# Loading the memory into the query projection's sum buffers, and two weighted values in another bank: a decoder block on one core

## The chip, the core and the metric

The kernel runs on one core of a Trainium2 chip. The core has a matrix engine (PE, which loads weights and multiplies), a vector engine (DVE), a scalar engine (ACT), GpSimd (POOL) and a sync engine (SP) that issues transfers. Each engine works its own instructions in order, and they meet at semaphores. Matrix results go to PSUM, eight banks of 128 x 512 float32; everything else lies in SBUF, 128 partitions wide. The metric is the device time of one execution in microseconds, less being better.

## The reference

One decoder block on 512 tokens of width 1024, in float32. A pooling mixer and a differential attention run on the same normed input, are gated and projected back (`w_out`). Then the tokens attend to a memory of 256 rows, and a squared-ReLU MLP follows. The part that the change touches:

```
x = x + mixed @ w_out[l]
hc = rms_norm(x, g_cross[l])
mem_n = rms_norm(mem, g_mem[l])
q = (hc @ w_cq).reshape(B, S, CROSS_HEADS, CROSS_HEAD_DIM)
kv = (mem_n @ w_ckv).reshape(B, M, 2, CROSS_HEADS, CROSS_HEAD_DIM)
k, v = kv[:, :, 0], kv[:, :, 1]
s = jnp.einsum('bshd,bmhd->bhsm', q, k) * CROSS_HEAD_DIM ** -0.5
p = jax.nn.softmax(s, axis=-1)
o = jnp.einsum('bhsm,bmhd->bshd', p, v).reshape(B, S, D_MODEL)
x = x + o @ w_co
```

with 4 heads of width 256.

## The kernel before

Activations lie transposed: 8 blocks of 128 features by 512 tokens. Every product is made from split operands: a value is rounded to a high part (`split`, line 116, a cast on ACT) and the remainder is a low part (line 117, a subtraction on DVE); `mm3` (lines 110 to 112) multiplies high by high, low by high and high by low. Weights pass through a ring: `load` fetches a block of 512 KB into one of three buffers `wraw` (SP's queue, line 154), `prep` splits it into `whi` and `wlo`, three buffers each, and PE multiplies. A block's split starts when PE has left the buffer three blocks earlier.

The order on PE is the order of the code. Work that belongs to a later moment is put off with `after(steps, fn)`: `tick` counts products, and `run_due` issues `fn` when its step has come. The order on ACT, DVE, POOL and SP is set by a scheduler from the code and its own estimates; each of these engines then works strictly in that order. Tags such as `tmp` (10 buffers) or `mraw` (3 in the middle part) are rings of buffers: a new tile waits until the work on the one that it replaces has ended.

The stages around the change:

- The output projection (`projection("out", ...)`): eight blocks of `wm`, m = 0 to 7. The first three sums lie in the banks `sc` and take five of their eight products early; `settle` stands between: it closes the pool of the attention's tiles, opens the pool of the middle part (tags `mraw` and `mfac`) on the same space, loads the residual rows `res` (tag `vr`) and puts off `mem_in` by 16 steps. The blocks 3 to 7 use the two banks `acc` in turn; `done_out` adds a sum to its residual row (`residual`, line 584, the eviction that frees the bank) and squares it (`accumulate`, lines 265 to 269).
- `mem_in`: the memory in four pieces of 2 x 256 columns. Each is scaled by the gain into a high part (line 272, ACT) and a low part (line 273, DVE), in buffers `s`, and its squares are summed (`ssm`, lines 265 to 269). The sum is split, and 20 steps later `stats` sums it over the partitions on PE (`rstd_full`, lines 242 and 243, and `rstd_rows`, lines 257 and 258) and takes the inverse root.
- `mem_k` and `mem_v`: keys and values of the memory, with the blocks of `wckv`.
- `cross_query`: the query projection by a seven-product scheme; some of its weights are sums of blocks, which `load` makes by one load on SP into `mraw` and a second, accumulating one on POOL (line 170).
- `cross_scores`, `cross_transpose`, `cross_out` by head. `cross_out(h)` makes two weighted values (dc = 0, 1), each summed in a bank over the memory's two halves, and splits each into `xg` (the eviction). PE does heads 1, 0, 3 in a row, with head 2's scores and head 3's transposes between 1 and 0; head 2's values follow inside the following projection (`w_co`).

The bank `av` (one) holds sums of the value projection and of the attention; nothing uses it after the attention.

Of the kernel before, what the change touches and what calls it, by code (L numbers as in the profile page):

```python
# [17 lines left out]
P = 128  # L18
T = 512
D = 1024  # L20
# [31 lines left out]
def block_kernel(ctx: ExitStack, tc: tile.TileContext, x0g, xT, memT, wv, wm, wst, wcq, wdn, wckv, wpool, vecs, csts, idn, gfin, out):  # L52
    nc = tc.nc
# [16 lines left out]
    def nm(s):  # L70
        uid[0] += 1
        return f"{s}_{uid[0]}"
# [6 lines left out]
    def sb(tag, shape, bufs, dt=F32):  # L79
        if tag in MID_TAGS and not late:  # L80
            return mid["pool"].tile(shape, dt, tag=tag, name=nm(tag), bufs=bufs)
        p = apool if tag in EARLY_TAGS else late["pool"] if tag in LATE_TAGS else pool
        return p.tile(shape, dt, tag=tag, name=nm(tag), bufs=bufs)

    def tmp(dt=F32):
        return sb("tmp", [P, T], 10, dt)
# [4 lines left out]
    def pair(tag, bufs):  # L91
        return sb(tag, [P, 2, T], bufs, F32R)

    def ps(tag, bufs):
        return psum.tile([P, T], F32, tag=tag, name=nm(tag), bufs=bufs)

    def acc():
        return ps("acc", 2)
# [10 lines left out]
    def mm3(o, lh, ll, rh, rl, start, stop):  # L109
        nc.tensor.matmul(o, lh, rh, start=start, stop=False)  # L110
        nc.tensor.matmul(o, lh, rl, start=False, stop=False)  # L111
        nc.tensor.matmul(o, ll, rh, start=False, stop=stop)  # L112


    def split(hi, lo, src, eng=V):
        S.copy(hi, src)  # L116
        eng.tensor_tensor(lo, src, f(hi), op=ALU.subtract)  # L117
# [117 lines left out]
    def split_sq(sq, w, eng=V):  # L235
        hi = tmp(F32R)[:, :w]
        lo = tmp(F32R)[:, :w]
        split(hi, lo, sq, eng)
        return hi, lo
# [5 lines left out]
    def rstd_full(sp, scratch, w=T):  # L245
        o = ps("tr", 2)[:, :w]
        bcast_sum(o, *sp)
        r = sb("rstd", [P, w], 1) if w == T else sb("mrstd", [P, w + 48], 1)[:, :w]
        rsqrt(r, o, 1.0 / D, scratch, tmp()[:, :w])
        return r  # L250

    def rstd_rows(sp, n):
        hi, lo = sp
        o = ps("tr", 2)
        for i in range(n):
            c = slice(i * P, (i + 1) * P)
            nc.tensor.matmul(o[:, 2 * i:2 * i + 2], hi[:, c], ones[:, :2], start=True, stop=False)
            nc.tensor.matmul(o[:, 2 * i:2 * i + 2], lo[:, c], ones[:, :2], start=False, stop=True)
        r = sb("rrow", [P, 16], 2)[:, :2 * n]
        rsqrt(r, o[:, :2 * n], 1.0 / D, sb("rscr", [P, 8], 4)[:, :2 * n], sb("rscr", [P, 8], 4)[:, :2 * n])  # L260
        return r

    def accumulate(ss, k, src, w=T):
        if k == 0:
            S.activation(ss, src, AF.Square)
        else:
            sq = tmp()[:, :w]
            S.activation(sq, src, AF.Square)
            V.tensor_tensor(ss, ss, sq, op=ALU.add)

    def scaled(hi, lo, src, g):
        S.activation(hi, src, AF.Copy, scale=g)
        V.scalar_tensor_tensor(lo, src, g, f(hi), op0=ALU.mult, op1=ALU.subtract)
# [5 lines left out]
    def after(steps, fn, *args):  # L279
        heapq.heappush(due, (clock[0] + steps, uid[0], fn, args))  # L280
        uid[0] += 1
# [11 lines left out]
    def flush():  # L293
        while due:
            clock[0] = max(clock[0], due[0][0])
            run_due()
# [48 lines left out]
    st = {}  # L345
# [258 lines left out]
    def mem_in():  # L604
        mg = {}
        sm = sb("ssm", [P, M], 1)
        for k2 in range(KC // 2):
            t = tmp()
            nc.gpsimd.dma_start(t, memT[:, 2 * k2:2 * k2 + 2, :])
            pr = pair("s", 6)  # L610
            for kk in range(2):
                k = 2 * k2 + kk
                c = slice(kk * M, (kk + 1) * M)
                scaled(pr[:, 0, c], pr[:, 1, c], t[:, c], vec[:, G_MEM + k:G_MEM + k + 1])
                accumulate(sm, k, t[:, c], M)
                mg[k] = (pr[:, 0, c], pr[:, 1, c])
        st["mg"] = mg
        sp = split_sq(sm, M)

        def stats():  # L620
            st["mrstd"] = rstd_full(sp, sm, M)
            st["mrow"] = rstd_rows(sp, MT)

        after(STATM, stats)
# [97 lines left out]
    def settle():  # L722
        flush()
        early.close()
        mid["pool"] = middle.enter_context(tc.tile_pool(name="mid", bufs=1))
        for m in range(KC):
            res[m] = sb("vr", [P, T], 8)
            nc.sync.dma_start(res[m], xT[:, m, :])
        after(MEMIN, mem_in)

    projection("out", mixed, EARLY, LATE, done_out, settle)
    sp1 = split_sq(ss1, T)

# [46 lines left out]
    def cross_out(h):  # L780
        pt = st["pt", h]
        for dc in range(2):
            o = acc()
            m = 2 * h + dc
            c = slice((m % 4) * P, (m % 4) * P + P)
            for i in range(MT):
                vh, vl = st["mv", m // 4, i]
                mm3(o, vh[:, c], vl[:, c], pt[0][:, i, :], pt[1][:, i, :], i == 0, i == MT - 1)
            pr = pair("xg", 8)
            split(pr[:, 0, :], pr[:, 1, :], o)  # L790
            cross_o[m] = (pr[:, 0, :], pr[:, 1, :])
# [90 lines left out]
    flush()  # L882
    cross_scores(3, "sc", 3)
    cross_out(1)
    cross_scores(2, "sc", 3)
    cross_transpose(3)
    cross_out(0)
    cross_out(3)
    after(2, cross_transpose, 2)
    after(7, cross_out, 2)  # L890
# [206 lines left out]
```

## Time and profile before

| | |
|---|---|
| runs | 720.0, 724.2 and 723.87 us, median 723.87 |
| profiled execution | 721.91 us, its span 720.1 us |
| granted TensorE clock, mean | 0.997 |
| moved by transfers | 94.78 MB, 132 GB/s in the mean |

The profile records one execution. Its times are microseconds from the span's start; a row of the timeline has start, length, engine, line, operation, the tile written and those read, and in brackets how long the engine had been idle and what ended that. A line is often that of a helper, so the tiles tell which step a row belongs to. `SPq` is a transfer's issue; the transfer itself lasts longer, up to its landing.

### The profile page before, as it was taken

To read this page: it belongs to the slowest core of one execution; us is meant where nothing else is said; L and a number is where in the kernel's file an instruction comes from. 1 tells how busy PE (TensorE), PEld (TensorE's weight loads), DVE (VectorE), ACT (ScalarE), POOL (GpSimd) and SP (SyncE) were. 2 spreads that over 40 slices of the span, in tenths; PEclk is the share of its full clock that TensorE was granted. 3 is DMA by queue.
4 is the path that set the end of the run, shared out by engine and by line. 5 is a ranking of instruction groups with operands and counts; after the bars stand their busy time and mean duration, and the time that the engine had idled before them with its cause. 6 is when DMAs were issued, how large, how long until landed. Compare 5 with 4: busy or idle time off the path is not lost.

```text
span 720.1 us, 10711 instructions
## 1 busy us (share of the span) xinstructions
PE 706.0 (98%) x4108; PEld 619.9 (86%) x4108; DVE 506.2 (70%) x818; ACT 425.1 (59%) x719; POOL 72.5 (10%) x67
## 2 busy tenths in 40 slices
PE   8999999999999999999999999999999999999995
PEld 6888788788879889997889988899889998899884
DVE  7597989986397989893786953688337864478633
ACT  7398998677376864572668742377215752257522
POOL 0044111634200000000100000000000000000000
PEclk9999999999999999999999999999999999999998
DMA  8433133134934436222934652168315672043211
GB/s 315 152 118 117 61 102 117 59 103 162 268 115 153 166 129 178 76 88 91 269 108 118 200 152 87 45 191 240 112 59 168 138 250 87 29 119 118 87 59 58
DMA packets 28130, 94.78 MB, mean 132 GB/s; under 512 B 3216, under 2 KB 3344, under 8 KB 28080
## 3 DMA queue, kind: packets, MB, share of 16 engines
q1 hardware_dynamic: 24688, 82.18, 33.1%
q0 software_dynamic: 3248, 11.67, 8.8%
q8 instruction: 32, 0.52, 0.3%
q10 hardware_dynamic: 144, 0.26, 0.1%
q14 instruction: 18, 0.15, 0.1%
HBM read 89.90 MB, written 2.10 MB: 128 GB/s over the span
## 4 chain that ended last, share of the span: by engine, by line
PE 81%; ACT 7%; DVE 6%; DMA 3%; issue 2%; POOL 1%; SPq 0%; DVEq 0%; POOLq 0%; ACTq 0%
PE acc L110 11%; PE acc L112 11%; PE acc L111 11%; PE sc L110 10%; PE sc L112 10%; PE sc L111 10%; PE tr L110 4%; PE tr L112 4%; PE tr L111 4%; DMA tmp<-memT 2%; ACT whi L116 1%; PE sc L397 1%; ACT tmp L459 1%; PE sc L399 1%; DVE wlo L117 1%
## 5 line engine op out<-in xcount | busy, mean ns | idle before, releaser
L116 ACT CAST whi<-wraw 128x1024 fp32r<-128x1024 f32 (+1 forms) x88 | 91.1, 1035 | 98.8 <-PE tr L112 50.8
L117 DVE TENSOR_TENSOR wlo<-wraw,whi 128x1024 fp32r<-128x1024 f32 (+1 forms) x88 | 108.1, 1228 | 39.8 <-ACT whi L116 38.4
L110 PE MATMUL acc<-xg,whi 128*128 128x512 f32 x200 | 80.1, 401 | 0.0
L112 PE MATMUL acc<-xg,wlo 128*128 128x512 f32 x200 | 78.2, 391 | 0.0
L111 PE MATMUL acc<-xg,whi 128*128 128x512 f32 x200 | 77.9, 390 | 0.0
L807 DVE TENSOR_TENSOR tmp<-sc,tmp 128x512 f32<-128x512 f32 x70 | 47.2, 687 | 11.4 <-PE sc L112 11.0
L110 PE MATMUL sc<-mix,whi 128*128 128x256 f32 (+1 forms) x184 | 54.8, 298 | 0.0
L116 ACT CAST whi<-mraw 128x1024 fp32r<-128x1024 f32 x34 | 35.5, 1050 | 32.6 <-PE sc L111 11.0
L112 PE MATMUL sc<-mix,wlo 128*128 128x256 f32 (+1 forms) x184 | 54.1, 294 | 0.0
L111 PE MATMUL sc<-mix,whi 128*128 128x256 f32 (+1 forms) x184 | 54.0, 293 | 0.0
L117 DVE TENSOR_TENSOR wlo<-mraw,whi 128x1024 fp32r<-128x1024 f32 x34 | 41.3, 1222 | 11.2 <-ACT whi L116 10.9
L170 POOL DMA_DIRECT2D mraw<-wst x16 | 13.8, 862 | 332.6 <-DMA mraw<-wst 203.1
L934 DVE SCALAR_TENSOR_TENSOR vr<-acc,sums,vr 128x512 f32<-128x512 f32 x16 | 12.0, 751 | 50.1 <-PE acc L112 50.1
L112 PEld LDWEIGHTS acc<-xg,wlo 128*128 128x128 f32 x200 | 37.5, 188 | 8.3
L110 PEld LDWEIGHTS acc<-xg,whi 128*128 128x128 f32 x200 | 37.6, 188 | 7.1
L111 PEld LDWEIGHTS acc<-xg,whi 128*128 128x128 f32 x200 | 37.7, 188 | 7.0
L116 ACT CAST mhl<-wraw 128x1024 fp32r<-128x1024 f32 x18 | 18.9, 1052 | 38.5 <-PE tr L111 27.4
L112 PEld LDWEIGHTS sc<-mix,wlo 128*128 128x128 f32 x184 | 34.6, 188 | 1.1
L110 PEld LDWEIGHTS sc<-mix,whi 128*128 128x128 f32 x184 | 34.6, 188 | 1.0
L111 PEld LDWEIGHTS sc<-mix,whi 128*128 128x128 f32 x184 | 34.5, 187 | 1.1
L117 DVE TENSOR_TENSOR mhl<-wraw,mhl 128x1024 fp32r<-128x1024 f32 x18 | 22.0, 1224 | 13.8 <-ACT mhl L116 13.8
L110 PE MATMUL sc<-s,whi 128*128 128x256 f32 x112 | 31.4, 281 | 0.0
(321 smaller groups left out, 2163.6 us busy)
## 6 DMA issues: line engine op xcount, KB each, us to landing
wraw<-wm SPq DMA_DIRECT2D x36, 512.0 KB, 3.3
wraw<-wdn SPq DMA_DIRECT2D x32, 512.0 KB, 5.0
mraw<-wst SPq DMA_DIRECT2D x24, 512.0 KB, 4.5
wraw<-wckv SPq DMA_DIRECT2D x16, 512.0 KB, 3.2
mraw<-wst POOLq DMA_DIRECT2D x16, 512.0 KB, 6.9
wraw<-wst SPq DMA_DIRECT2D x16, 512.0 KB, 3.2
mraw<-wcq SPq DMA_DIRECT2D x6, 512.0 KB, 3.9
s<-s SPq DMA_DIRECT2D x8, 256.0 KB, 3.7
```

Of the source, the lines that this page charges most:

```text
L110: nc.tensor.matmul(o, lh, rh, start=start, stop=False)
L111: nc.tensor.matmul(o, lh, rl, start=False, stop=False)
L112: nc.tensor.matmul(o, ll, rh, start=False, stop=stop)
L116: S.copy(hi, src)
L117: eng.tensor_tensor(lo, src, f(hi), op=ALU.subtract)
L170: nc.gpsimd.dma_start(r, part(key, then), accum_op=ALU.add)
L397: nc.tensor.matmul(o[i], xg[k][0][:, tb], wh[:, c], start=k == 0, stop=False)
L399: nc.tensor.matmul(o[i], xg[k][1][:, tb], wh[:, c], start=False, stop=False)
L459: S.activation(e[:, :n], e[:, :n], AF.Exp, bias=mn, scale=-1.0, accum_out=sm[:, c:c + 1])
L807: V.tensor_tensor(u[new], o, u[old], op=ALU.add)
L934: V.scalar_tensor_tensor(y, o, sums[:, 2 * NT + t:2 * NT + t + 1], y, op0=ALU.mult, op1=ALU.add)
```

## The change

The memory's transposed input is loaded in two pieces of 512 KB instead of four of 256 KB. The loads are issued from `settle`, on SP's queue, into two buffers of the tag `mraw`, instead of from `mem_in`, on POOL's queue, into four buffers `tmp`. `mem_in` takes its pieces from those two. And `cross_out` puts the first value of head 0 and the second of head 3 into the bank `av`, the other six into the banks `acc` as before.

```diff
@@ mem_in
         for k2 in range(KC // 2):
-            t = tmp()
-            nc.gpsimd.dma_start(t, memT[:, 2 * k2:2 * k2 + 2, :])
+            t = st["mem"][k2 // 2][:, k2 % 2 * T:(k2 % 2 + 1) * T]
             pr = pair("s", 6)
@@ settle
             nc.sync.dma_start(res[m], xT[:, m, :])
+        st["mem"] = [sb("mraw", [P, D], 3) for _ in range(2)]
+        for j, t in enumerate(st["mem"]):
+            nc.sync.dma_start(t, memT[:, 4 * j:4 * j + 4, :])
         after(MEMIN, mem_in)
@@ cross_out
-            o = acc()
+            o = ps("av", 1) if (h, dc) in ((0, 0), (3, 1)) else acc()
```

What it does to the order of the engines' work, at three places. In the rows, a tile's number tells its buffers apart and has no other meaning; it differs between the two kernels for the same tile, and line numbers of the changed kernel are up to three higher or lower. `x2` stands for two equal instructions in a row.

First, SP's queue in the output projection. Before:

```order
L154 DMA wraw_1845<-wm 128x1024
L154 DMA wraw_1867<-wm 128x1024
L154 DMA mraw_2693<-wcq 128x1024
L154 DMA mraw_2734<-wcq 128x1024
L154 DMA mraw_2795<-wcq 128x1024
L154 DMA wraw_1947<-wm 128x1024
L154 DMA wraw_2037<-wm 128x1024
L154 DMA wraw_2072<-wckv 128x1024
```

Now:

```order
L154 DMA wraw_1845<-wm 128x1024
L154 DMA wraw_1867<-wm 128x1024
L730 DMA mraw_1909<-memT 128x1024
L730 DMA mraw_1910<-memT 128x1024
L154 DMA mraw_2689<-wcq 128x1024
L154 DMA wraw_1951<-wm 128x1024
L154 DMA wraw_2033<-wm 128x1024
L154 DMA mraw_2730<-wcq 128x1024
L154 DMA wraw_2068<-wckv 128x1024
L154 DMA mraw_2791<-wcq 128x1024
```

The memory's loads stand where two of the three query weights stood; those two follow later, each ahead of a block of key weights. In both kernels the first load into `mraw` waits for the last work on the space that the pool takes over, a product of the gates on POOL (line 523). In the kernel now the second and third query weights reuse the memory's buffers, and so wait for ACT's last square of each.

Second, ACT from the last gated value (`mix`) on; `whi_1847`, `whi_1869` are the weights of the output blocks m = 3 and 4, the fourth and fifth. Before:

```order
L116 CAST mix_1819<-s_1679 128x512
L116 CAST whi_1847<-wraw_1823 128x1024
L265 ACTIVATE ss_1822<-vr_1893 128x512
L116 CAST whi_1869<-wraw_1845 128x1024
L268 ACTIVATE tmp_1930<-vr_1895 128x512
L116 CAST whi_1949<-wraw_1867 128x1024
L268 ACTIVATE tmp_1943<-vr_1897 128x512
L272 ACTIVATE s_1977<-tmp_1975,vx_67 128x256
L265 ACTIVATE ssm_1974<-tmp_1975 128x256
```

Now:

```order
L116 CAST mix_1819<-s_1679 128x512
L272 ACTIVATE s_1979<-mraw_1909,vx_67 128x256
L265 ACTIVATE ssm_1978<-mraw_1909 128x256
L272 ACTIVATE s_1979<-mraw_1909,vx_67 128x256
L272 ACTIVATE s_1988<-mraw_1909,vx_67 128x256 x2
L116 CAST whi_1847<-wraw_1823 128x1024
L272 ACTIVATE s_1999<-mraw_1910,vx_67 128x256 x2
L272 ACTIVATE s_2010<-mraw_1910,vx_67 128x256 x2
L265 ACTIVATE ss_1822<-vr_1893 128x512
L116 CAST whi_1869<-wraw_1845 128x1024
```

The memory's scaling has moved from behind three weight casts to ahead of the first of them. Seven of the eight squares of the memory are not in these rows: they come after the third cast, in one piece.

DVE, from the first eviction of the projection (`vr_1893`) on. Before:

```order
L584 TENSOR_TENSOR vr_1893<-sc_1829,vr_1893 128x512
L117 TENSOR_TENSOR wlo_1848<-wraw_1823,whi_1847 128x1024
L584 TENSOR_TENSOR vr_1895<-sc_1851,vr_1895 128x512
L117 TENSOR_TENSOR wlo_1870<-wraw_1845,whi_1869 128x1024
L269 TENSOR_TENSOR ss_1822<-ss_1822,tmp_1930 128x512
L584 TENSOR_TENSOR vr_1897<-sc_1873,vr_1897 128x512
L117 TENSOR_TENSOR wlo_1950<-wraw_1867,whi_1949 128x1024
L269 TENSOR_TENSOR ss_1822<-ss_1822,tmp_1943 128x512
L273 SCALAR_TENSOR_TENSOR s_1977<-tmp_1975,vx_67,s_1977 128x256
```

Now, from the memory's first low part on:

```order
L273 SCALAR_TENSOR_TENSOR s_1979<-mraw_1909,vx_67,s_1979 128x256 x2
L584 TENSOR_TENSOR vr_1893<-sc_1829,vr_1893 128x512
L273 SCALAR_TENSOR_TENSOR s_1988<-mraw_1909,vx_67,s_1988 128x256 x2
L117 TENSOR_TENSOR wlo_1848<-wraw_1823,whi_1847 128x1024
L273 SCALAR_TENSOR_TENSOR s_1999<-mraw_1910,vx_67,s_1999 128x256
L584 TENSOR_TENSOR vr_1895<-sc_1851,vr_1895 128x512
```

Four low parts of the memory and an eviction stand ahead of the low part of the fourth block's weights (`wlo_1848`); before, the memory's first low part came after six rows of weights and evictions and two of squares.

Third, ACT's evictions (`xg`) of the weighted values of heads 0 and 3, in the order of PE's products; ahead of them a high part of head 3's transposed weights (`mfac`) and an exponential of head 2. Before:

```order
L116 CAST mfac_3486<-tr_3495 128x2x256
L760 ACTIVATE tmp_3478,small_3476<-sc_3462,small_3475,rrow_2287 128x256 x2
L116 CAST xg_3509<-acc_3502 128x512
L116 CAST xg_3519<-acc_3512 128x512
L116 CAST xg_3529<-acc_3522 128x512
L116 CAST xg_3539<-acc_3532 128x512
```

Now:

```order
L116 CAST mfac_3482<-tr_3491 128x2x256
L762 ACTIVATE tmp_3474,small_3472<-sc_3458,small_3471,rrow_2283 128x256 x2
L116 CAST xg_3505<-av_3498 128x512
L116 CAST xg_3515<-acc_3508 128x512
L116 CAST xg_3525<-acc_3518 128x512
L116 CAST xg_3535<-av_3528 128x512
```

Nothing moves in the order here; two sums change their bank. With two banks `acc` in turn, head 3's first value stood in the bank of head 0's first; now it stands in that of head 1's second.

## The prediction

> **What bounds the kernel now.** I read the page first, then the list of PE's waits, then PE's timeline around each of them that the change can touch, then ACT, DVE, POOL and SP at those places. The first rows are of the page: span, busy time by engine, the chain by engine.
>
> ```profile
> span 720.1 us, 10711 instructions
> ...
> PE 706.0 (98%) x4108; PEld 619.9 (86%) x4108; DVE 506.2 (70%) x818; ACT 425.1 (59%) x719; POOL 72.5 (10%) x67
> ...
> PE 81%; ACT 7%; DVE 6%; DMA 3%; issue 2%; POOL 1%; SPq 0%; DVEq 0%; POOLq 0%; ACTq 0%
> ```
>
> PE is the bound: all that the other engines do can cost at most 720.1 - 706.0 = 14.1 us, start and end included. The chain gives 3% to DMA, and the one transfer of this change is 10.9 us of it; but a chain follows what was late, not what PE lost. What PE lost stands in its timeline (start, length, and in brackets the idle time with its releaser):
>
> ```profile
> 187.23 0.39 PE L110 MATMUL acc<-mix,whi 128*128 128x512 f32 x1
> ...
> 187.69 0.39 PE L112 MATMUL acc<-mix,wlo 128*128 128x512 f32 x1
> ...
> 197.99 0.40 PE L112 MATMUL acc<-mix,wlo 128*128 128x512 f32 x1
> 198.90 0.47 PE L110 MATMUL acc<-mix,whi 128*128 128x512 f32 x1 [0.52 <-DVE vr L584]
> 199.21 0.40 PE L111 MATMUL acc<-mix,whi 128*128 128x512 f32 x1
> ...
> 206.44 0.39 PE L112 MATMUL acc<-mix,wlo 128*128 128x512 f32 x1
> 207.46 0.38 PE L242 MATMUL tr<-tmp,ones 128*128 128x256 f32 x1 [0.63 <-ACT tmp L116]
> 207.96 0.38 PE L243 MATMUL tr<-tmp,ones 128*128 128x256 f32 x1
> ...
> 323.61 0.40 PE L112 MATMUL acc<-mfac,mix 128*128 128x512 f32 x1
> 324.88 0.50 PE L110 MATMUL acc<-mfac,mix 128*128 128x512 f32 x1 [0.87 <-DVE xg L117]
> 325.22 0.40 PE L111 MATMUL acc<-mfac,mix 128*128 128x512 f32 x1
> ```
>
> From 187.23 to 187.69 are two steps, so a 512-column matmul starts every 0.23 us (a 256-column one takes half, 0.12). Starts further apart than that are lost time: at 198.90, 0.91 - 0.23 and 0.31 - 0.23, together 0.76 us; at 207.46, 1.02 - 0.23 and 0.50 - 0.12, together 1.17 us; at 324.88, 1.27 - 0.23 and 0.34 - 0.23, together 1.15 us. These 3.08 us are all that the two edits can reach.
>
> Behind the first two stands one transfer. ACT and DVE, with POOL and SP:
>
> ```profile
> 178.12 1.29 POOL L523 TENSOR_TENSOR s<-s,gate 128x512 f32<-128x512 f32 x1
> ...
> 179.44 1.28 SPq L154 DMA_DIRECT2D mraw<-wcq  x3
> ...
> 184.73 1.78 POOL L170 DMA_DIRECT2D mraw<-wcq  x2 [3.29 <-DMA mraw<-wcq]
> 186.20 1.97 POOL L609 DMA_DIRECT2D tmp<-memT  x3
> ...
> DMA to landing us min/median/max: 10.9/11.7/12.0
> ...
> 197.12 0.51 ACT L272 ACTIVATE s<-tmp,vx 128x256 fp32r<-128x256 f32 x1 [7.79 <-DMA tmp<-memT]
> ...
> 198.07 0.68 DVE L584 TENSOR_TENSOR vr<-acc,vr 128x512 f32<-128x512 f32 x1
> ...
> 207.49 0.42 DVE L117 TENSOR_TENSOR tmp<-ssm,tmp 128x256 fp32r<-128x256 f32 x1
> ```
>
> The memory's loads (landing row: from a question on the tensor memT) stand on POOL behind two accumulating loads, which wait for a load from SP; SP's waits for POOL's last gate product, over at 179.41. So memT is issued at 186.20 and is there at 197.1. ACT idles 7.79 us for it; DVE's eviction of the output projection's fourth sum (L584) is behind the memory's work and ends at 198.75, and the sum of squares is split only at 207.49 to 207.91. PE asked at 198.22 (197.99 and a step) and 206.67.
>
> **The change part by part.** *Loads.* Two SP loads of 512 KB replace four of POOL's, on the place in SP's queue where three weight loads (mraw<-wcq) stood, and wait for the same product. So they leave at 179.44 and about 179.9. The nearest rows are those weight loads, the same queue, moment and size, asked for by the short windows in which each was issued, beside the transfers' share just ahead:
>
> ```profile
> 179.00:180.00 1.00, 1.00 (x6) 0.83 (x5) 0.00 (x0) 0.55 (x1) 0.41 (x1) 1.00 0.00 0
> ...
> DMA to landing us min/median/max: 3.5/3.5/3.5
> ...
> DMA to landing us min/median/max: 4.3/4.3/4.3
> ```
>
> Nothing else is in flight then (DMA share 0.00). The first lands at 179.44 + 3.5 = 182.94, the second near 184.2, against 197.1 now. Bounds: 3.5, and from far the 10.9 us of memT's own row, which was taken among other transfers. I take 3.5, the row that differs only in the tensor read.
>
> *What is queued behind the new wait.* ACT and DVE now do half of the memory's scaling ahead of the fourth block's weight cast and its low part, in front of which nothing waited on memory before. The paces:
>
> ```profile
> 183.31 0.69 DVE L584 TENSOR_TENSOR vr<-sc,vr 128x512 f32<-128x512 f32 x1 [6.33 <-PE sc L112]
> 184.17 1.23 DVE L117 TENSOR_TENSOR wlo<-wraw,whi 128x1024 fp32r<-128x1024 f32 x1 [0.17 <-ACT whi L116]
> ...
> 198.55 1.03 ACT L116 CAST whi<-wraw 128x1024 fp32r<-128x1024 f32 x1
> 199.49 0.51 ACT L272 ACTIVATE s<-tmp,vx 128x256 fp32r<-128x256 f32 x1
> 199.90 0.40 ACT L268 ACTIVATE tmp<-tmp 128x256 f32<-128x256 f32 x1
> 200.21 0.49 ACT L272 ACTIVATE s<-tmp,vx 128x256 fp32r<-128x256 f32 x1
> ...
> 205.43 0.48 DVE L273 SCALAR_TENSOR_TENSOR s<-tmp,vx,s 128x256 fp32r<-128x256 f32 x1
> 205.82 0.42 DVE L269 TENSOR_TENSOR ssm<-ssm,tmp 128x256 f32<-128x256 f32 x1
> ```
>
> Start to start, ACT spends 0.41 on a scaling (199.49 to 199.90), 0.31 on a square, 0.94 on a weight cast (198.55 to 199.49); DVE 0.39 on a low part of the memory (205.43 to 205.82) and, from its lengths, about 0.6 on an eviction and 1.14 on a weight's low part. From 182.94, ACT has scaling, square and three scalings, 4 x 0.41 + 0.31 = 1.95: the cast begins at 184.9 and ends at 185.95. DVE has the second low part after the second scaling (182.94 + 0.72 + 0.5 = 184.2), then the eviction that was free at 183.31 (184.6), two low parts (185.2 to 186.0), then the weight's low part, 186.0 to 187.25. PE wants the cast at 187.23 and the low part at 187.69. So no new wait, but the low part's margin shrinks from 187.69 - 185.40 = 2.3 us to 0.44. Each us that memT lands later than 3.9 us after its issue costs PE one.
>
> *The old waits.* From the cast's start ACT runs that cast, four scalings, a square of a residual row (about 0.5), two casts, two more such squares and the memory's seven other squares: 184.9 + 0.94 + 1.64 + 0.5 + 1.88 + 1.0 + 2.2 = 193.1. DVE runs from 186.0 three weight low parts, four of the memory, two evictions and four additions (0.34 to 0.6 each, say 1.9), 186.0 + 3.42 + 1.56 + 1.2 + 1.9 = 194.1, and then the fourth sum's eviction, done near 194.8; PE asks at 198.22. The sum of squares needs one more weight low part and five additions, near 197.6, and its split a us more; PE asks at 206.67 - 0.76 = 205.9. Margins of 3.4 and 7 us: both waits go, 0.76 + 1.17 = 1.93 us.
>
> *Behind the moved loads.* The two weight loads that are accumulated onto now wait in SP's queue until ACT has squared the memory (near 192 and 193), and the first key weights (wckv) stand behind them, so these leave near 193. They are cast when the sixth block frees its buffer, 187.23 + 3 x 24 x 0.23 = 203.8: the landing of 3.5 us leaves 7 us, that of 10.9 us none. The accumulated weights are used after the memory's keys and values, much later. POOL loses four issues, on nobody's path. All this costs nothing; the cover is those margins.
>
> *Banks.* The first weighted value of head 0 and the second of head 3 go to the bank "av", idle since the attention. PE's order is the same. What PE waited for at 324.88 is the low part of head 0's first value; what it also needs there:
>
> ```profile
> 318.53 0.69 DVE L117 TENSOR_TENSOR xg<-acc,xg 128x512 fp32r<-128x512 f32 x1
> ...
> 322.07 1.28 DVE L117 TENSOR_TENSOR mfac<-tr,mfac 128x512 fp32r<-128x512 f32 x2
> ...
> 324.14 1.28 DVE L117 TENSOR_TENSOR xg<-acc,xg 128x512 fp32r<-128x512 f32 x2
> ```
>
> Head 3's first value now takes the bank that was read out by 319.22; its operand is split by 323.35; so it starts at 323.84. Its second takes "av" 1.4 us later, at 325.2, after the first of the two evictions of 324.14 (done by 324.8). So the 1.15 us go, and I find nothing that is late next: the following product reads head 0's two values, ready by 325.42, at 323.84 + 12 x 0.23 = 326.6.
>
> The sum: 0.76 + 1.17 + 1.15 = 3.08 us less, nothing added. The profiled execution took 721.91 us (1.81 around its span), so 718.8; the median of the runs shown is 723.87, 1.96 above it, so 720.8 by that. Nothing tells which of the two the next runs are like, so I state the middle, 719.8.
>
> A rule that speaks against the first edit: the Trainium skill, "PSUM — Partial Sum Buffer", Engine vs sequencer instructions, has ScalarE's and VectorE's queues as strict FIFO. The 7.79 us idle ahead of the L272, with a weight cast behind it, agrees; by that rule alone the new place of the memory's work is a risk to PE from the 0.44 us on, and with the landing of 3.5 us the sum stays 3.08.
>
> **The rivals.** *Slower: memT lands late.* If its loads take 10.9 us as now, the low part is 10.9 - 3.5 - 0.44 = 7.0 us late and PE stands for it at 187.69; with 3.08 gained, 721.91 + 3.9 = 725.8 (727.8 from the median). It decides from 3.9 + 3.1 = 7.0 us on. For it: the row of 10.9. Against it: that row had other transfers beside it, this place has none. *Part of that*: a landing between 3.9 and 7.0 us eats some of the gain: 719 to 722. *The move does nothing*: the memory's waits come back in another form, and only the bank's 1.15 us stay: 720.8 (722.7). For it: every wait here was under 1.3 us, as small as an order's side effects; against it the margins of 3.4 and 7 us. By the Trainium skill, "DMA: Bandwidth & Descriptors", Issuing engines are not separate DMA queues, loads of all issuers share the same 16 engines and another issuer saves only its issue time; by that rule a change of issuer would be this rival. The trace agrees that contention is shared (10.9 us on POOL beside SP's loads), but here the issue itself comes 6.8 us sooner.
>
> **How the numbers follow.** Forecast (all three waits gone) 0.62, part eaten 0.15, move without effect 0.15, slower 0.08. Low end: the fastest run 720.0 less 3.1 is 716.9, set to 716.5. High end: the slowest run 724.2, with next to nothing gained, set to 724.0; beyond it lies the slower rival and little else. A measurement of this kernel tells about 1%, 7.2 us, from no change; every case above, the worst at +3.9 and the best at -3.1, lies inside. So same 0.96, faster 0.02, slower 0.02.
>
> **What would show it.** Right: memT issued on SP near 179.4 and landed near 183; no PE wait on L584 or L242 around 198 and 206; none on xg at 324, with a span near 717. Wrong: a PE wait on wlo or whi at 187 to 188 (the margin was misjudged), a first landing beyond 3.9 us, a key weight that PE waits for at 216, or a new wait where PE reaches the next projection sooner.

## The result, and the profile after

| | before | after |
|---|---|---|
| median of 10 runs each | 721.6 us | 717.56 us (716.64 to 720.09) |
| ratio | | 0.9946, 95% interval 0.9928 to 0.9964 |
| profiled execution | 721.91 us, span 720.1 | 717.47 us, span 715.7 |

The time is 2.6 to 5.2 us shorter by the interval, about half a per cent, which counts as no change by the bound of 1%. It is 2.2 us below the 719.8 of the forecast and inside its range.

First the page of the changed kernel: span and instructions, busy time by engine, the chain by engine.

```profile
span 715.7 us, 10711 instructions
...
PE 703.5 (98%) x4108; PEld 619.1 (87%) x4108; DVE 506.6 (71%) x818; ACT 424.5 (59%) x719; POOL 70.3 (10%) x63
...
PE 85%; ACT 6%; DVE 4%; issue 2%; DMA 1%; POOL 1%; SPq 0%; DVEq 0%; ACTq 0%
```

PE is still the bound. The chain gives DMA 1% instead of 3%, since the transfer of 10.9 us has left it, and what it and the other engines lost there PE has gained, 81 to 85%.

Next the timelines of SP, ACT, DVE and PE of the changed kernel where the memory comes in, with the landing row of the tensor memT (start, length, and in brackets the idle time and what ended it).

```profile
177.51 0.80 SPq L730 DMA_DIRECT2D mraw<-memT  x2
...
DMA to landing us min/median/max: 4.2/4.7/5.1
...
181.81 0.51 ACT L272 ACTIVATE s<-mraw,vx 128x256 fp32r<-128x256 f32 x1 [3.67 <-DMA mraw<-memT]
...
183.74 1.03 ACT L116 CAST whi<-wraw 128x1024 fp32r<-128x1024 f32 x1
...
184.85 1.22 DVE L117 TENSOR_TENSOR wlo<-wraw,whi 128x1024 fp32r<-128x1024 f32 x1
...
185.53 0.39 PE L111 MATMUL acc<-mix,whi 128*128 128x512 f32 x1
186.13 0.50 PE L112 MATMUL acc<-mix,wlo 128*128 128x512 f32 x1 [0.21 <-DVE wlo L117]
186.46 0.39 PE L110 MATMUL acc<-mix,whi 128*128 128x512 f32 x1
```

The first load lands 4.2 us after its issue, not 3.5. ACT, which works in order, comes to the fourth block's weight cast (183.74) only behind four scalings and a square of the memory, DVE's low part of that weight ends at 186.07, and PE, which would have started at 185.76, starts at 186.13. Counted as in the prediction, 0.60 - 0.23 and 0.33 - 0.23, PE loses 0.47 us here: a new, small wait, at a place that the prediction names among its signs of being wrong.

Then PE of the changed kernel where the three old waits stood, and the two instructions of DVE behind which the first two were.

```profile
196.54 0.39 PE L112 MATMUL acc<-mix,wlo 128*128 128x512 f32 x1
196.77 0.40 PE L110 MATMUL acc<-mix,whi 128*128 128x512 f32 x1
...
204.09 0.39 PE L112 MATMUL acc<-mix,wlo 128*128 128x512 f32 x1
204.32 0.28 PE L242 MATMUL tr<-tmp,ones 128*128 128x256 f32 x1
204.44 0.28 PE L243 MATMUL tr<-tmp,ones 128*128 128x256 f32 x1
...
320.00 0.40 PE L112 MATMUL acc<-mfac,mix 128*128 128x512 f32 x1
320.23 0.39 PE L110 MATMUL acc<-mfac,mix 128*128 128x512 f32 x1
...
192.91 0.69 DVE L584 TENSOR_TENSOR vr<-acc,vr 128x512 f32<-128x512 f32 x1
...
197.25 0.43 DVE L117 TENSOR_TENSOR tmp<-ssm,tmp 128x256 fp32r<-128x256 f32 x1 [0.47 <-ACT tmp L116]
```

Each start follows the one before it by a step, 0.23 us (0.12 for 256 columns), and no bracket stands behind it: the three waits are gone. (The product at 320.23 is the first of head 3's first value, the one that stood at 324.88 before.) The eviction of the fourth sum ends at 193.60, 3.2 us before PE asks; the sum of squares is split at 197.68, 6.6 us before.

The two spans differ by 4.4 us, more than the three waits were worth. Part of it has nothing to do with the change. The first float32 products of the two executions, the kernel before and then the changed one, in two fences, each with the first pair of transposes of line 475, some 70 us later:

```profile
5.50 1.62 PE L397 MATMUL sc<-whi,xg 128*128 128x512 f32 x3 [0.71 <-DVE whi L203]
...
7.35 1.48 PE L399 MATMUL sc<-whi,xg 128*128 128x512 f32 x3
...
9.06 1.04 PE L401 MATMUL sc<-wlo,xg 128*128 128x512 f32 x3
...
72.73 0.41 PE L475 MATMUL tr<-ident,tmp 128*128 128x128 f32 x2 [0.35 <-DVE tmp L464]
```

```profile
5.12 1.22 PE L397 MATMUL sc<-whi,xg 128*128 128x512 f32 x3 [0.33 <-DVE whi L203]
...
6.41 0.86 PE L399 MATMUL sc<-whi,xg 128*128 128x512 f32 x3
...
7.33 0.84 PE L401 MATMUL sc<-wlo,xg 128*128 128x512 f32 x3
...
70.81 0.41 PE L475 MATMUL tr<-ident,tmp 128*128 128x128 f32 x2 [0.34 <-DVE tmp L464]
```

In the first the groups of three last 1.62 and 1.48 us, half the later pace, up to 9 us; in the second the later pace (0.84) is reached at 6.4 us. The pair comes at 72.73 and 70.81, so 1.92 of the 4.4 us lie ahead of everything that the change touches. From there to the end the spans take 647.37 and 644.89 us: 2.5 us for the change. Which of this belongs to the kernels and which to the executions is what the runs had to tell.

At the other end of the span the change loses a little, in no wait of PE. SP's last issue of an output, in the kernel before, in the changed kernel, and in the one of the experiments whose memory loads POOL issues (e3_pool_issue, span 715.0):

```profile
716.45 0.33 SPq L956 DMA_DIRECT2D out<-vr  x1
...
711.72 0.33 SPq L958 DMA_DIRECT2D out<-vr  x1
...
711.37 0.33 SPq L958 DMA_DIRECT2D out<-vr  x1
```

From there to the span's end pass 3.6, 4.0 and 3.6 us. All seven profiles with the memory's loads on SP have 3.95 to 3.99 here, the seven others 3.58 to 3.62. In the trace SP ends the program with ten checks of transfers, 0.06 us each; the one that waits for this output is the ninth in the kernel before and the third in the changed one, so six more come behind it, which makes up the 0.38 us between 3.60 and 3.98. The prediction has no term for this. Why the check's turn moves with the loads was not traced.

### The profile page after: what moved, and what is told of

Read it like the earlier page. It is cut to its first block, busy times and chain, and to the rows that moved or that the text cites. A ratio compares the mean times of both kernels' runs of the same rounds, so it can differ in the third digit from the quotient of the medians.

```text
span 715.7 us, 10711 instructions
## 1 busy us (share of the span) xinstructions
PE 703.5 (98%) x4108; PEld 619.1 (87%) x4108; DVE 506.6 (71%) x818; ACT 424.5 (59%) x719; POOL 70.3 (10%) x63
## 4 chain that ended last, share of the span: by engine, by line
PE 85%; ACT 6%; DVE 4%; issue 2%; DMA 1%; POOL 1%; SPq 0%; DVEq 0%; ACTq 0%
PE acc L110 12%; PE acc L112 12%; PE acc L111 11%; PE sc L110 11%; PE sc L112 11%; PE sc L111 10%; PE tr L112 4%; PE tr L110 4%; PE tr L111 4%; ACT whi L116 1%; ACT tmp L459 1%; PE sc L397 1%; DVE wlo L117 1%; DMA mraw<-wcq 1%; PE sc L399 1%
```

## The experiments

Twelve runs were made in three groups; those of a group share one chip and the runs of the kernel before, whose medians there were 721.3 (29 runs), 721.76 (17) and 721.27 us (23). "Loss" below is counted as in the prediction, start to start beyond a step.

**Each edit alone, and the kernel before against itself** (first group)

`e1_mem_only` is the kernel before with the memory's edit and without the bank's:

```diff
-            o = ps("av", 1) if (h, dc) in ((0, 0), (3, 1)) else acc()
+            o = acc()
```

> The memory's loads moved as in the change, the banks as before. Theory (each edit is worth what PE's timeline loses at its places, and the rest of the 4.4 us between the two profiled spans is a slower start of the profiled execution of before): no PE wait near 196 and 205, a wait of 0.2 to 0.4 us near 186, the wait on xg near 322 back with 1.0 to 1.3 us; in time 1.5 us less than before, ratio 0.998. Rival (the memory's move is also worth something that no wait shows): 2.5 us or more less, ratio 0.9965 or lower.

718.81 us, ratio 0.9976 (0.9962 to 0.9991), which is 0.6 to 2.7 us less; the mean of its 12 runs is 1.9 us below that of the kernel before, and the two waits that it should remove were 1.93. The medians lie 2.5 us apart, so the time alone excludes neither the theory's ratio of 0.998 nor the rival's 0.9965. Its landing row, and its PE at the bank:

```profile
DMA to landing us min/median/max: 3.8/4.3/4.9
...
322.38 0.40 PE L112 MATMUL acc<-mfac,mix 128*128 128x512 f32 x1
323.64 0.50 PE L110 MATMUL acc<-mfac,mix 128*128 128x512 f32 x1 [0.86 <-DVE xg L117]
```

The waits near 198 and 207 are gone (those products come a step behind the ones before them, at 198.67 and 206.22), that on `xg` stands as it was, and with a landing of 3.8 us no wait on `wlo` is listed (the two steps there lose 0.07 us).

`e2_bank_only` is the other half: the kernel before with the bank's edit alone.

```diff
-            o = acc()
+            o = ps("av", 1) if (h, dc) in ((0, 0), (3, 1)) else acc()
```

> The two banks alone, the memory loaded as before. Theory: the waits near 198 and 207 stand as before (0.5 and 0.6 us), the one on xg near 324 is gone and nothing takes its place; 1.15 us less, ratio 0.9984. Rival (the time saved is lost again at PE's next wait, near 383): ratio 1.000. Rival (more than the wait is saved): ratio below 0.997.

720.65 us, ratio 0.9994 (0.9985 to 1.0004): between 1.1 us less and 0.3 more, the mean 0.9 us less, against 1.15 forecast. The time by itself doesn't settle it; the trace does: no wait on `xg`, nothing in its place, and the memory's two waits as in the kernel before.

```profile
196.57 0.40 PE L112 MATMUL acc<-mix,wlo 128*128 128x512 f32 x1
197.49 0.47 PE L110 MATMUL acc<-mix,whi 128*128 128x512 f32 x1 [0.52 <-DVE vr L584]
197.79 0.40 PE L111 MATMUL acc<-mix,whi 128*128 128x512 f32 x1
...
206.04 0.38 PE L242 MATMUL tr<-tmp,ones 128*128 128x256 f32 x1 [0.75 <-ACT tmp L116]
```

From line 475 to the end its span takes 646.2 us, against 647.4 to 648.3 in the four profiles with both old stages, so the gain is not lost again later. By the traces each edit takes away its own waits, with or without the other.

`e4_null` is the kernel before without an edit.

> The kernel before, once more, as a measure of the start. Theory: ratio 1.000 within 0.15%; the start is the execution's and not the kernel's: PE's first float32 matmuls (from 5 us on) run either 0.43 us apart up to about 9 us, as in the profile of before, or 0.23 us apart from about 6 us, as in the profile after, which makes about 1.9 us of difference at the first transposes near 71 us. Rival (the start belongs to the kernel): the slow start again, with the transposes at 72.7 us, and the kernels with the memory moved always at 70.8.

721.51 us, ratio 1.0003 (0.9987 to 1.0019). Its profile has the pair of line 475 at 70.96 us, as early as the changed kernel's, and two of those with the memory moved have it late (73.13 in e1_mem_only, 72.72 in e6_run512), so the start belongs to the execution and not to the kernel. And the memory costs more here than in the profile on which the prediction rests:

```profile
195.94 0.51 ACT L272 ACTIVATE s<-tmp,vx 128x256 fp32r<-128x256 f32 x1 [8.43 <-DMA tmp<-memT]
...
196.18 0.40 PE L112 MATMUL acc<-mix,wlo 128*128 128x512 f32 x1
197.72 0.47 PE L110 MATMUL acc<-mix,whi 128*128 128x512 f32 x1 [1.14 <-DVE vr L584]
198.02 0.40 PE L111 MATMUL acc<-mix,whi 128*128 128x512 f32 x1
...
206.27 0.39 PE L242 MATMUL tr<-tmp,ones 128*128 128x256 f32 x1 [0.75 <-ACT tmp L116]
206.76 0.39 PE L243 MATMUL tr<-tmp,ones 128*128 128x256 f32 x1
```

1.54 - 0.23 and 0.30 - 0.23 are 1.38, and at 206.27 another 1.28 (1.14 - 0.23 and 0.49 - 0.12): 2.66 us in place of 1.93.

**A landing that should be later**

`e6_run512` is the changed kernel with the memory laid out so that each partition's part of a load comes in runs of 512 bytes instead of one of 4 KB; the engines' order is that of the change.

```diff
-            nc.sync.dma_start(t, memT[:, 4 * j:4 * j + 4, :])
+            nc.sync.dma_start(t.rearrange("p (c m) -> p c m", c=8),
+                              memT[8 * j:8 * j + 8].rearrange("c p m -> p c m"))
...
-        "memT": i["mem"][0].reshape(M, KC, P).transpose(2, 1, 0),
+        "memT": i["mem"][0].reshape(2, 128, KC, P).transpose(2, 0, 3, 1).reshape(16, P, 128),
```

> The changed kernel with the memory laid out so that its two loads read runs of 512 bytes instead of 4 KB, every engine's order as in the change: the first memory load lands later, by an amount X that the trace gives (estimate 1 to 4 us, from the 4.2 us now up to what smaller transfers took). Theory (the low part of the fourth block's weights is behind the memory's scaling, with no margin left): PE's wait near 186 grows from 0.37 us to 0.37 + X, and the time by X. Rival (other work hides the landing): the wait stays under 0.5 us whatever X.

717.43 us, ratio 0.9949 (0.9936 to 0.9962). The estimate was wrong: the landing is not later.

```profile
DMA to landing us min/median/max: 3.6/4.1/4.7
```

So this run didn't test what a really late landing would cost. It is still a point of use: 3.6 us, and no loss at `wlo`.

**Who issues the loads, and which comes first** (second group)

`e3_pool_issue` has them issued by POOL, at the same place in the program:

```diff
-            nc.sync.dma_start(t, memT[:, 4 * j:4 * j + 4, :])
+            nc.gpsimd.dma_start(t, memT[:, 4 * j:4 * j + 4, :])
```

> The changed kernel with the two memory loads issued by GpSimd instead of SyncE, at the early place (the program's end of the output projection's set-up, which in GpSimd's order is right behind its last gate product at about 177 us, ahead of the query weights). Theory (what took the waits away is that the loads stand ahead of the query weights and need no later buffer, not who issues them): landing 3.5 to 6 us after issue, no wait on the eviction at 198 us and none on the squares at 206 us, time within 0.7 us of the change: 717.2 to 718.2 us. Rival (GpSimd's issue itself is slow to land, 10.9 to 12 us as in the kernel before): the first scaling on ScalarE at about 189 us, TensorE waits near 198 us as before or more, time 720 us or above.

716.8 us, ratio 0.9928 (0.9916 to 0.994). Its POOL, landing row and ACT:

```profile
177.90 1.12 POOL L730 DMA_DIRECT2D mraw<-memT  x2 [0.31 <-POOL s L523]
...
DMA to landing us min/median/max: 6.1/6.4/6.7
...
181.25 1.06 ACT L116 CAST whi<-wraw 128x1024 fp32r<-128x1024 f32 x1 [3.01 <-PE sc L111]
...
184.05 0.51 ACT L272 ACTIVATE s<-mraw,vx 128x256 fp32r<-128x256 f32 x1 [1.74 <-DMA mraw<-memT]
```

The same issuer as in the kernel before, and none of the old waits (PE's products there come at 196.39 and 203.94, a step behind the ones before them); the rival "it is the issuer" falls. What remains of the change is the loads' place, ahead of the query weights instead of behind them, with their buffers and their size of 512 KB; these three were not tried apart. POOL's landing is 2 us longer than SP's, and it costs nothing, since here the order puts the fourth weight's cast (181.25) ahead of the scalings. The Trainium skill, "DMA: Bandwidth & Descriptors", Issuing engines are not separate DMA queues, has all issuers feed the same 16 transfer engines, so that another issuer saves only the time of issuing; that the waits go with either issuer fits this, but no run here shows the sharing by itself, and the 2 us between the landings are more than the issue times differ (1.12 us for two loads on POOL, 0.80 on SP).

`e5_swap` is the change with the two loads issued in the other order:

```diff
-        for j, t in enumerate(st["mem"]):
-            nc.sync.dma_start(t, memT[:, 4 * j:4 * j + 4, :])
+        for j in (1, 0):
+            nc.sync.dma_start(st["mem"][j], memT[:, 4 * j:4 * j + 4, :])
```

> The changed kernel with the two memory loads issued in the other order, so that the blocks 0 to 3, which the scalings read first, come second; by the order of the instructions the cast of the fourth output block's weight (whi) and its low part (wlo) then stand ahead of the memory's scalings on ScalarE and VectorE. Theory (the wait of 0.21 us on wlo at 186 us, a slip of 0.37 us, comes from the cast standing behind a scaling that waits for the first load): no wait of TensorE on wlo or whi near 186 us, the old waits near 198, 207 and 324 us stay away, and the time is the change's less 0 to 0.4 us: 717.0 to 717.6 us, ratio to the kernel before 0.9935 to 0.995. Rival (the scalings, now some 0.5 us later, bring a wait back near 198 or 207 us): a wait of 0.3 us or more there, time 717.8 to 718.5 us.

717.09 us, ratio 0.9934 (0.9921 to 0.9947). ACT and PE of it:

```profile
181.18 1.06 ACT L116 CAST whi<-wraw 128x1024 fp32r<-128x1024 f32 x1 [3.00 <-PE sc L111]
182.88 0.51 ACT L272 ACTIVATE s<-mraw,vx 128x256 fp32r<-128x256 f32 x1 [0.65 <-DMA mraw<-memT]
...
185.56 0.39 PE L111 MATMUL acc<-mix,whi 128*128 128x512 f32 x1
185.78 0.39 PE L112 MATMUL acc<-mix,wlo 128*128 128x512 f32 x1
```

The cast stands first, PE goes from 185.56 to 185.78 without a pause, and no old wait is back: the change's new wait came from the order of ACT's and DVE's work, as the prediction's step on it has it. Its time can't be told from the change's, 0.47 us away.

**The start of the kernel**

`e8_warm` is the change with ten instead of eight warm-up products (products at the start whose result nothing uses), `e9_warm_before` the kernel before with the same edit:

```diff
-WARM = 8
+WARM = 10
```

> The changed kernel with ten instead of eight warm-up matmuls, nothing else. In six profiled executions the first float32 matmul waited 0 to 1.00 us for whi (line 203) behind the warm-up; where TensorE then stood still for 0.54, 0.62 and 0.71 us its matmuls ran 0.43 us apart until 9 to 10 us, where it stood still for 0 and 0.33 us only until about 5.7 us. Theory (a gap behind the warm-up sets the pace back): with ten the warm-up ends at about 5.6 us, no gap; the first transposes (line 475) come at 70.8 to 71.6 us in the profile instead of 70.8 to 73.1, and the time is 716.3 to 717.3 us with a smaller spread; executions that had no gap lose up to 0.7 us, so a gain of 0.2 to 1 us at the median. Rival (the pace at the start has nothing to do with the gap): two more matmuls cost up to 0.7 us, time 717.5 to 718.3 us.

717.57 us, ratio 0.9939 (0.9926 to 0.9952), inside the rival's range. No gain over the change's 717.56 and 717.99 (below); the theory that closing the gap behind the warm-up pays has no support in the time, although the profiled execution started earliest of all (line 475 at 70.31 us). Two other profiles speak against the gap as the cause: e2_bank_only and e3_pool_issue stood still for 1.00 and 0.98 us and had the pair of line 475 at 71.33 and 70.88. What the pace does follow is the trace's record of the granted clock (last section).

> The kernel before with ten instead of eight warm-up matmuls. If the start's pace is what the difference of 4.0 us between the medians holds beyond the 2.5 to 3.1 us that the traces of the change account for, both kernels with ten warm-up matmuls should stand 2.5 to 3.1 us apart (this one 719.3 to 720.5 us). If the remaining 1 us is in the memory's stall (which measured 1.9 us in one profiled execution and 2.6 us in another), they stay 3.5 to 4 us apart (this one 720.3 to 721.3 us). Waits near 198, 206 and 324 us as in the kernel before in either case.

720.98 us, ratio 0.9989 (0.998 to 0.9997), 3.41 above e8_warm. Two points of it are to be seen, at ACT and at PE:

```profile
195.93 0.51 ACT L272 ACTIVATE s<-tmp,vx 128x256 fp32r<-128x256 f32 x1 [8.75 <-DMA wraw<-wckv]
...
195.83 0.40 PE L112 MATMUL acc<-mix,wlo 128*128 128x512 f32 x1
197.70 0.47 PE L110 MATMUL acc<-mix,whi 128*128 128x512 f32 x1 [1.48 <-DVE vr L584]
198.01 0.39 PE L111 MATMUL acc<-mix,whi 128*128 128x512 f32 x1
```

1.72 us are lost here and 1.30 near 206: 3.02 in all, the largest stall of any profile. (The bracket of the first row names a weight's transfer, but the instruction reads `tmp` and `vx`; the releaser is inferred, and here it is put down to another transfer than the memory's.) The distance of 3.41 us lies between the two forecasts, 2.5 to 3.1 and 3.5 to 4 us, so the times don't decide. The two profiles do, for themselves: their spans differ by 3.6 us (718.9 and 715.3), of which 0.24 lie ahead of line 475 (70.55 and 70.31). In this pair the distance is in the stages of the change and not in the start.

`e10_cold_before` and `e11_cold_after` are the opposite, two warm-up products (third group):

```diff
-WARM = 8
+WARM = 2
```

> The kernel before with two instead of eight warm-up matmuls, nothing else: TensorE stands still for about 3 us ahead of its first float32 matmul, so in each execution its start should be slow, and the first float32 transposes behind the opening projection (line 475, tr<-ident,tmp at 72.73 us in the profile of the kernel before, 70.55 to 71.33 in those of three other executions of its memory stage) should come at 72.5 to 73.5 us. Theory (the memory's transfers are not paced by TensorE alone: the first scaling came at 197.12 us behind a slow start and at 195.71 to 195.94 behind fast ones, so a late TensorE waits less for it): TensorE's slips near 198 and 207 us sum to 1.5 to 1.9 us instead of 2.6 to 2.9, and the time grows by 0 to 1 us only: 721.5 to 722.8 us. Rival (the stall has a size of its own that varies by chance): slips of 1.9 to 2.9 us, and the time grows by all of the 1.5 to 2 us that the start loses: 723.0 to 723.8 us.

722.69 us, ratio 1.0017 (1.0006 to 1.0028). The time is inside the theory's 721.5 to 722.8, but the growth of 1.4 us lies between the theory's 0 to 1 and the rival's 1.5 to 2. The start was not as late as expected either (line 475 at 71.65 us). PE:

```profile
196.88 0.40 PE L112 MATMUL acc<-mix,wlo 128*128 128x512 f32 x1
198.18 0.47 PE L110 MATMUL acc<-mix,whi 128*128 128x512 f32 x1 [0.90 <-DVE vr L584]
198.49 0.40 PE L111 MATMUL acc<-mix,whi 128*128 128x512 f32 x1
```

The stall is 1.15 and 1.29 us, 2.44 in all: above the theory's 1.5 to 1.9 and within the rival's 1.9 to 2.9.

> The changed kernel with two instead of eight warm-up matmuls. Nothing in the memory's stage waits for a transfer here by more than 0.4 us, so a slow start should be lost in full by both theories: line 475 at 72.5 to 73.5 us, no waits near 198, 207 and 324 us, time 719.0 to 719.8 us. Theory of e10_cold_before: the two kernels with two warm-ups stand 2.2 to 3.2 us apart; its rival: 3.7 to 4.3 us apart.

719.20 us, ratio 0.9969 (0.9957 to 0.9981), in the 719.0 to 719.8 that both theories share, with line 475 at 72.44 us. It is 3.49 us below e10_cold_before, between the two forecasts of 2.2 to 3.2 and 3.7 to 4.3. No wait near 198, 207 or 324. As a test between "a late start hides part of the stall" and "the stall varies by itself" the pair is inconclusive: both kernels lost nearly the same by the cold start, 1.4 us and 1.2 to 1.6 (against 717.99 and 717.56), which speaks against more than a small part being hidden.

**Two repeats**

`e12_after_again` is the changed kernel, `e13_pool_again` that of e3_pool_issue, without a further edit.

> The changed kernel once more, on the same chip as the next run, for a second profile of it. 716.6 to 718.2 us. By the threshold of 3.9 us: if its first memory load lands later than 4.0 us after its issue, a slip of 0.2 to 0.5 us at the low part of the weight near 186 us, if it lands earlier, none.

717.99 us, ratio 0.9954 (0.9936 to 0.9971). With a landing of 4.0 us the products at `wlo` start at 186.06, 186.51 and 186.85, a loss of 0.33 us.

> The memory loads issued by GpSimd at the early place once more, beside the changed kernel on the same chip. If its 716.8 us (five runs within 0.3 us) was a gain over the change, it stands 0.3 to 0.8 us below it here as well, with no wait on wlo near 186 us; if it was the executions', the two are within 0.3 us. Its landing of 6.1 us again without a wait, since here the cast of the weight stands ahead of the scalings.

717.91 us, ratio 0.9946 (0.9927 to 0.9966), beside 717.99. So the time of 716.8 did not come again, and by their times none of the variants is better than the change itself. The traces see more, once the start is left out. From line 475 to the end the two profiles with POOL's loads take 644.1 us each (715.0 - 70.88 and 717.2 - 73.12). The five of the changed kernel, of e6_run512 and with other warm-ups, take 644.9 to 645.8: 0.4 us of the difference are SP's end of the program, 0 to 0.47 the wait at `wlo`, and up to 1.05 us the waits on exponentials of the last section. The start, 2.3 us from the earliest to the latest with eight warm-ups, hides this in the times.

**What the stall of the kernel before depends on.** The five profiles that have the old memory stage:

| profile | line 475 | first scaling (ACT, L272) | from one to the other | PE's loss near 198 and 207 |
|---|---|---|---|---|
| e2_bank_only | 71.33 | 195.71 | 124.38 | 2.05 |
| before | 72.73 | 197.12 | 124.39 | 1.93 |
| e10_cold_before | 71.65 | 196.40 | 124.75 | 2.44 |
| e4_null | 70.96 | 195.94 | 124.98 | 2.66 |
| e9_warm_before | 70.55 | 195.93 | 125.38 | 3.02 |

Over these five the loss follows, about one for one, when the memory lands as counted from PE's own progress. In the mean it is 2.42 us, and the profile that the prediction was made from has the smallest. Why the landing moves by 1.0 us against PE was not traced further.

## Why the prediction was right, and where its sizes were off

*The forecast.* Within 1% and faster by a few us: right, by the likeliest case.

*Old waits, 0.76 and 1.17 us.* Both gone in every kernel with the early loads, and e1_mem_only alone removes them. The mechanism is right; the margins of 3.4 and 7 us measured 3.2 and 6.6. The size is that of one execution: five measure 1.93 to 3.02.

*Banks, 1.15 us.* Right: the wait goes with this edit alone, is there without it, and nothing takes its place. Its loss is the same in e1_mem_only as before (1.26 - 0.23 and 0.34 - 0.23).

*First load landing 3.5 us after issue, nothing added.* This is the term that failed, and two of the prediction's signs of being wrong came with it, the landing beyond 3.9 us and the wait on `wlo`: 4.2 us in the profile of the change, 3.6 to 4.2 in the seven with SP's loads. With the limit of 3.9 the loss should have been 0.3 us; it was 0.47. By landing, in the profiles with this order of the engines: none at 3.6, 0.07 at 3.8, 0.28 to 0.35 at 4.0 (three profiles), 0.47 at 4.2. So the slope of one is supported from 3.8 to 4.2 us, and the limit lies near 3.7, 0.2 us lower than worked out. The path itself was well priced: from the first scaling's start to the low part's end it was to take 4.31 us (182.94 to 187.25) and took 4.26 (181.81 to 186.07). What the limit left out is 0.06 us from the low part's end to PE's start and the 0.10 us that PE's next product comes late, which the prediction does count for the old waits. The Trainium skill, "PSUM — Partial Sum Buffer", Engine vs sequencer instructions, has ScalarE's and VectorE's queues as strict FIFO; this wait agrees: ACT takes up the cast at 183.74, behind the memory's scalings, while in e5_swap, where it stands ahead of them, the same cast starts at 181.18.

*Behind the moved loads.* Right. The first key weight leaves at 191.21, which with the start 1.92 us earlier is the 193 forecast, and PE waits for none.

*The sum.* 3.08 us forecast, with nothing added. In the two profiles 1.93 + 1.15 went, 0.47 came at `wlo`, and 0.38 at the end of the program, a place that the prediction does not look at: 2.23 us of the 2.48 measured behind line 475. The other 0.25 are in the memory's stage too, from the product that starts at 195.01 us before to the one at 212.07, 17.06 us, now 14.88: products right behind the counted ones also came late. With the stall's mean, 2.42 + 1.15 less 0.28 to 0.47 and 0.38 is 2.7 to 2.9 us. The medians of four pairs differ by 4.0 (before and after), 3.3 (e12_after_again), 3.4 (ten warm-ups) and 3.5 us (two). That leaves 0.4 to 1.3 us by medians that no term names. The interval of the first pair, 1.3 us to either side, just covers it, and the start varies by more. So the sum came out near the measured gain partly by luck: a stall larger than in the one profile made up for the two terms that were missing.

*The time, 719.8 us.* Most of the 2.2 us by which it was too high are the base. That was 722.9, the middle between the profiled 721.91 and 723.87, a median of three runs; the kernel before has its median at 721.3 to 721.8 in larger samples.

*The rivals.* "Memory lands late" did not come; what it would cost beyond 4.2 us in this order of the engines was not measured, and e3_pool_issue shows that with the cast first even 6.1 us is free. "Part eaten" did come, as a loss of 0.28 to 0.47 us in four of the six profiles with this order. "The move does nothing" is out by e1_mem_only.

## What to carry to other kernels

A load that lies on the path behind others can be made early by a place ahead of them in the queue, into buffers that are free by then. Who issues it did not decide whether the waits went, but it has its own small prices: 2 us of landing on POOL, 0.4 us at the end of the program on SP. Work that is moved forward takes its place in the engines' order too: what now stands behind it (here a weight's cast) has to be priced with the landing's spread, not with one landing. And a stall read from one profile is one draw: here it ranged from 1.9 to 3.0 us between executions of the same stage, so a gain of a few tenths of a per cent deserves more than one profile of the kernel before.

## What the runs showed of the hardware

- The pace at the start differs between executions of the same program: after the same eight warm-up products, products of 512 columns came to 0.23 us apart at about 6 us in one execution and past 9 us in another. The view's granted clock reads 1.00 for both stretches, but the trace's record of the clock has no entry that early: its first one, full clock, begins at 9.46 us in the kernel before and at 5.74 in the changed one. In the ten profiles with eight warm-ups it begins at 3.9 to 10.4 us. Wherever this is later than the first product, in all 14 profiles, the pace of 0.23 us is reached within 0.2 us behind it. The pair of line 475 came at 70.8 to 73.1 us in the profiles with eight warm-ups. The Trainium skill, "TensorE: Matmul & The Clock Gate", The HAM clock gate, has the clock decided by an activity window that runs freely against the kernel's start, so that the change to full speed falls differently from run to run; the spread agrees in kind, and the full-clock entries of the 14 profiles last 703.15, 706.56 or 709.97 us, 3.41 us apart, as whole windows of one length would.
- Loads of 512 KB from SP in runs of 512 bytes landed no later (3.6 us, one profile) than in runs of 4 KB (3.8 to 4.2 us, six profiles).
- The same loads took 5.7 and 6.1 us from POOL and 3.6 to 4.2 from SP, at the same place of the program.
- Waits of 0.17 to 0.34 us on ACT's exponentials (`tmp`, near 288 to 293 us) stand in five profiles of both kinds of kernel and are missing in the others. Where they stand, the stretch around them is 0.4 to 1.05 us longer; they were not explained.
